# An order set by hand for VectorE, ScalarE, GpSimd and the loads in the paired output projection

## The chip, the cores and the metric

The kernel runs on one core of a Trainium2 chip. Its metric is device time in microseconds (us) of one execution. The core has TensorE (PE, the matrix unit), VectorE (DVE), ScalarE (ACT), GpSimd (POOL) and SyncE (SP, which here issues nearly all transfers); each runs its own instructions in order. On-chip data lie in SBUF, matrix results in PSUM, everything else in device memory.

## The reference

One encoder layer on 2048 tokens of width 1024: a modulated norm and a projection feed an attention branch and an mLSTM branch; their normed outputs are concatenated and go through one output projection into a gated residual; then comes a SwiGLU feed-forward with a second gated residual, and a last norm. The part this case is about, cut to what matters:

```python
att = rms_norm(att, g_attn_out)                                # width 512
h_m = sigmoid(o_m) * rms_norm(h_fwd + h_bwd, g_mlstm_out)      # width 512
mix = concatenate([att, h_m], axis=-1) @ w_out                 # 1024 x 1024
x = x + gate1 * mix
hff = rms_norm(x, g_norm2) * (1.0 + scale2) + shift2
gte, up = split(hff @ w_ffn_in, 2, axis=-1)
ff = (silu(gte) * up) @ w_ffn_out
return x + gate2 * ff
```

All values are 32-bit floats. A product of the kernel is made of three matrix instructions, on a high and a low part of each operand.

## The kernel before, in words

**Seven products instead of eight.** The output projection takes token tiles of 128 in pairs (8 pairs). A pair of tiles is seen as a 2 by 2 block matrix, tile by half of the 1024 input channels, and multiplied by the weight's four blocks in Strassen's manner: seven products u0 to u6 instead of eight. Each has four k-steps of three matmuls (lines 56, 57 and 58, tile `ops`), so a pair has 84 matmuls and 28 steps i. Three PSUM banks hold the results: u0, u2, u4 and u6 add into one (b1), u1 has its own (b2), u3 and u5 share the third (b5). After each product VectorE adds the bank to the residual row `xr` (L1033). A later product into the same bank may start only when that addition has read it: u2 waits for u0's addition, u4 for u2's, u6 for u4's, u5 for u3's.

**What a pair needs.** `Pair(p)` loads the pair's attention outputs twice (`msq`, to be squared, and `ma`), the mLSTM outputs (`mm`) and, in `load_gate`, the output gate (`og`). `sums` squares `msq` on ScalarE (L972) and sums it in two GpSimd steps (L973, L974); `root` has TensorE add over channels (tile `aps`, L980) and VectorE make the inverse root (nine short instructions and L983); `scale` has TensorE spread it (tile `arb`) and VectorE scale `ma` (L990); `gate` multiplies `mm` (L993). `operands` makes the seven left operands mA11, mA12, mS2, mS1, mS3, mS4 and mA22: four GpSimd sums or differences (L1006, L1007, L1012, L1015), and for each operand a ScalarE copy, the high part (L1001), and a VectorE subtraction, the low part (L1002). While pair p is multiplied, pair p+1 is scaled and its operands are made, and pair p+2 is loaded, squared and rooted.

**Ahead of the pairs** lies the fill: the products of the mLSTM output gate (`o_tiles`, L417, tile `gps`, copied to `oth` and stored to `og_d`), between which the first two pairs are prepared; `pull(n)` takes n of its steps. The output weights' seven products (`wo`, two tiles each for high and low) are loaded and finished there too (L889 load, L890 ScalarE copy, L891 VectorE subtraction).

**Beside the pairs** runs `norm2`, the second norm, for four token tiles at a time (in pairs 2, 3 and 4, 5, 6): it loads the new residual rows (`x1t`) that the pairs before have stored (L1037), squares them (`junk`, L1081), makes the inverse roots (`rs`), scales (L1086), transposes them on TensorE (`trn`, L162; ScalarE makes `n` from them, L163), and stores blocks to device memory (`hop_d`). The second group (z = 1) loads the first group's blocks back and stores their sums. In pair 7 `refill_ops` loads these blocks as the feed-forward's right operands (tiles `B` and `T`, finished at L1127 and L1128), and `weights` makes the feed-forward's first left operands (L1166, L1167). Then the feed-forward begins (tile `fp`; ScalarE copies `s` at L1263 and `u` at L1269 free its banks).

**What sets the order.** TensorE's order is written by hand, in the order of the program text, from the second half of the kernel on. VectorE, ScalarE, GpSimd and SP have theirs from the scheduler of the tile framework, which sets it at build time by its own costs. SP's queue is in order as well: a transfer that waits for its slot holds those behind it, and each transfer has to wait for the eighth before it.

Of the kernel before, what the change touches and what calls it, by code (L numbers as in the profile page):

```python
# [21 lines left out]
P = 128  # L22
# [14 lines left out]
def hybrid_layer_kernel(  # L37
# [844 lines left out]
    wo = []  # L882

    def load_wo(us):
        for u in us:
            hl = [[big(4 * u + 2 * z + i, "wo") for i in range(2)] for z in range(2)]
            for i in range(2):
                hi, lo = hl[0][i], hl[1][i]
                sp.dma_start(lo.bitcast(F32), wo_d[u, 2 * i:2 * i + 2].rearrange("k p t -> p k t"))  # L889
                act.activation(hi, lo.bitcast(F32), AF.Copy)  # L890
                dve.tensor_tensor(lo, lo.bitcast(F32), hi.bitcast(F32), SUB)  # L891
            wo.append(hl)
# [6 lines left out]
    for s_ in range(len(order) + 2):  # L899
# [24 lines left out]
        if len(wo) < 4 and s_ > 31 and lasts[len(wo) // 2] not in fill:  # L924
            load_wo(range(len(wo), len(wo) + 2))
    assert next(wops, None) is None
    finish_fill(lasts[1])
    load_wo(range(len(wo), 4))
# [21 lines left out]
    class Pair:  # L950


        def __init__(self, p):
            self.tt = tt = TO[2 * p]
            v = lambda t: t.rearrange("p i k t -> p (i k) t")
            self.sq = mring_tile("msq", F32).rearrange("p i (k t) -> p i k t", k=4)
# [11 lines left out]

        def sums(self):

            sq = self.sq
            act.activation(sq, sq, AF.Square)  # L972
            pool.tensor_tensor(sq[:, :, 0:2], sq[:, :, 0:2], sq[:, :, 2:4], ADD)  # L973
            pool.tensor_tensor(sq[:, :, 0], sq[:, :, 0], sq[:, :, 1], ADD)  # L974
# [20 lines left out]
        def operands(self):  # L995
# [9 lines left out]
            s2_ = xp.tile([P, 512], F32, tag="n2", name="ms2", bufs=5)  # L1005
# [33 lines left out]

    nxt = Pair(0)  # L1040
    nxt.load_gate()
    xr = [load_xr(nxt.tt + i) for i in range(2)]
    nxt2 = Pair(1)
    nxt.sums()
    nxt.gate()
    nxt2.load_gate()
    pull(36)
    finish_fill(lasts[1])
    nxt.root()
    nxt2.sums()  # L1050
    pull(18)
    nxt.scale()
    ready = nxt.operands()
    next(ready), next(ready), next(ready)
    finish_fill(lasts[2])
    load_wo(range(4, 6))
    pull(10)
# [3 lines left out]
    load_wo(range(6, 7))  # L1061
    deque(ready, 0)
# [5 lines left out]
    def norm2(hh, z, tags, lead):  # L1068
# [15 lines left out]
        yield True  # L1084
        for i in range(4):
            act.activation(xt[i], xt[i], AF.Copy, scale=r[:, i:i + 1])  # L1086
            yield True
        if z == 0:
            for k in range(KT):
                t = new()  # L1090
                turned(t, xt, k, tags[k % 2], gs2, mod[:, 3, :])
                sp.dma_start(op["B11" if k < 4 else "B21"][k % 4], t)
                yield True
        else:
            done = ()
            for k in range(4):
                for o, t in done:
                    sp.dma_start(op[o][k - 1], t)
# [5 lines left out]
                turned(b22, xt, k + 4, tags[1], gs2, mod[:, 3, :])  # L1104
                e.tensor_tensor(t3, b22, b12, SUB)
                dve.tensor_tensor(b12, b12, b11, SUB)
                dve.tensor_tensor(b11, b22, b12, SUB)
                e.tensor_tensor(b21, b21, b11, SUB)
                done = (("B22", b22), ("T3", t3), ("T1", b12), ("T2", b11), ("T4", b21))
                yield True  # L1110
            yield True
            for o, t in done:
                sp.dma_start(op[o][3], t)

    def refill_ops(hh):
# [14 lines left out]
        def after(u):  # L1130
            start(u)
            if u > 1:
                finish(u - 2)
# [3 lines left out]
    ring = deque([("big", "big28")] + [("w", f"w{i}{z}") for i in range(2) for z in "hl"]  # L1137
                 + [("big", f"big{i}") for i in range(29, 32)] + [("ff", f"r{i}") for i in range(4)])
# [20 lines left out]
    def weights(raw, early=False):  # L1159

        w11, w12, s2_, s1_, s3_, s4_, w22 = (ring_tile(n) for n in ("A11", "A12", "S2", "S1", "S3", "S4", "A22"))
        g, a21, a22 = raw
        a11, a12 = g[:, :512], g[:, 512:]

        def part(t, f):
# [7 lines left out]
        part(w11, a11)  # L1173
        part(w12, a12)
        part(s1_, f1)
        pool.tensor_tensor(a21, a11, a21, SUB)
        part(s2_, f2)
# [383 lines left out]
```

## Time and profile before

| | us |
|---|---|
| median of 3 runs | 2414.3 (2413.35 to 2416.13) |
| the profiled execution | 2406.27 |
| its span in the profile | 2404.5 |
| TensorE busy | 2265.9 |
| the eight pairs, first product to last | 883.8 to 1086.4 |

All times in the profile count from the start of the span. A row of the instruction view is start, length, engine, line, operation, output and inputs, shape, and in brackets how long the engine stood idle before it and whose work ended that. "SPq" is the issue of a transfer. The rows of waits give engine and line, what was waited for, and total, times and longest. A duration of a matmul row is longer than the spacing of two matmuls, since they overlap.

### The profile page before, as it was taken

What the parts mean: (1) busy time and instruction counts of PE and PEld (TensorE: products, weight loads), DVE (VectorE), ACT (ScalarE), POOL (GpSimd) and SP (SyncE); (2) the same over time, 40 slices, a digit from 0 to 9 for tenths busy, and PEclk for the clock granted to TensorE, in tenths of its full rate; (3) what the DMA queues carried; (4) which work ended last, traced back from release to release, by engine and by line L of the source; (5) the groups of instructions that cost most, each with busy time, mean ns of one, the idle gap of its engine ahead of it and who ended that gap; (6) DMA issues with size and microseconds to landing.
All of it is one profiled execution on the core that took longest, in us unless ns stands there. A gap on an engine that the chain in (4) does not pass through costs nothing.

```text
span 2404.5 us, 32677 instructions
## 1 busy us (share of the span) xinstructions
PE 2265.9 (94%) x10801; PEld 1874.7 (78%) x10801; DVE 1565.9 (65%) x3096; ACT 1061.2 (44%) x2133; POOL 1024.1 (43%) x874
## 2 busy tenths in 40 slices
PE   5988999999999978987999999999999999999998
PEld 4987777788787857766888888788888888888886
DVE  6774677767687756667555567756565537684684
ACT  4522555544577733435345344533344423223452
POOL 1001234334466332434655655555656545492020
PEclk9999999999999989998999999999999999999999
DMA  7573455576788576865334345633333264442452
GB/s 291 175 242 105 132 160 160 170 213 186 220 253 255 164 239 205 265 244 179 105 110 167 97 143 182 210 100 112 102 107 105 88 206 157 150 161 97 141 199 89
DMA packets 363522, 401.86 MB, mean 167 GB/s; under 512 B 24670, under 2 KB 255576, under 8 KB 363352
## 3 DMA queue, kind: packets, MB, share of 16 engines
q1 hardware_dynamic: 363352, 399.78, 52.5%
q8 instruction: 85, 1.39, 0.3%
q14 instruction: 85, 0.70, 0.1%
HBM read 280.50 MB, written 119.19 MB: 166 GB/s over the span
## 4 chain that ended last, share of the span: by engine, by line
PE 50%; DVE 4%; DMA 4%; POOL 3%; issue 2%; ACT 2%; SPq 1%; POOLq 0%; ACTq 0%; DVEq 0%
PE fp L56 11%; PE fp L57 11%; PE fp L58 11%; PE fo L58 5%; PE fo L56 5%; PE fo L57 5%; DMA msq<-mxa_d 1%; PE ops L56 1%; DVE al L1346 1%; PE gps L417 1%; DMA al<-a_d 1%; PE ops L57 1%; PE ops L58 1%; POOL ms L1007 0%; POOL ma L1006 0%
## 5 line engine op out<-in xcount | busy, mean ns | idle before, releaser
L417 PE MATMUL gps<-hT,whi 128*128 128x512 f32 x1088 | 401.7, 425 | 8.6 <-ACT ctanh L431 7.8
L56 PE MATMUL fo<-w,ah 128*128 128x512 f32 x616 | 242.2, 393 | 2.6 <-ACT ah L1345 2.6
L58 PE MATMUL fo<-w,al 128*128 128x512 f32 x616 | 242.4, 393 | 0.2 <-DVE al L1346 0.2
L57 PE MATMUL fo<-w,ah 128*128 128x512 f32 x616 | 241.9, 393 | 0.0
L417 PEld LDWEIGHTS gps<-hT,whi 128*128 128x128 f32 x1088 | 204.6, 194 | 35.9 <-ACT ctanh L431 8.5
L417 PE MATMUL gps<-hT,wlo 128*128 128x512 f32 x544 | 230.7, 424 | 0.0
L56 PE MATMUL fp<-T,S 128*128 128x512 f32 x528 | 210.0, 398 | 15.5 <-ACT s L1263 9.9
L57 PE MATMUL fp<-T,S 128*128 128x512 f32 x528 | 208.2, 394 | 0.0
L58 PE MATMUL fp<-T,S 128*128 128x512 f32 x528 | 208.2, 394 | 0.0
L1346 DVE TENSOR_TENSOR al<-al,ah 128x1024 fp32r<-128x1024 f32 x77 | 114.4, 1490 | 134.2 <-ACT ah L1345 133.9
L1167 DVE TENSOR_TENSOR A<-graw,A 128x512 fp32r<-128x512 f32 x86 | 105.4, 1246 | 108.0 <-ACT A L1166 108.0
L1345 ACT ACTIVATE ah<-al 128x1024 fp32r<-128x1024 f32 x77 | 81.6, 1060 | 193.8 <-DMA al<-a_d 184.7
L56 PEld LDWEIGHTS fo<-w,ah 128*128 128x128 f32 x616 | 115.8, 188 | 28.9 <-ACT ah L1345 3.0
L58 PE MATMUL fp<-B,A 128*128 128x512 f32 x352 | 137.6, 391 | 0.0
L56 PE MATMUL fp<-B,A 128*128 128x512 f32 x352 | 137.6, 391 | 0.0
L57 PE MATMUL fp<-B,A 128*128 128x512 f32 x352 | 137.6, 391 | 0.0
L58 PEld LDWEIGHTS fo<-w,al 128*128 128x128 f32 x616 | 115.8, 188 | 27.7 <-DVE al L1346 1.4
L57 PEld LDWEIGHTS fo<-w,ah 128*128 128x128 f32 x616 | 115.9, 188 | 26.4
L56 PEld LDWEIGHTS fp<-T,S 128*128 128x128 f32 x528 | 100.3, 190 | 39.3 <-ACT s L1263 10.8
L1167 DVE TENSOR_TENSOR S<-sf,S 128x512 fp32r<-128x512 f32 x86 | 87.5, 1019 | 55.9 <-ACT S L1166 55.8
L58 PEld LDWEIGHTS fp<-T,S 128*128 128x128 f32 x528 | 100.1, 190 | 22.6
L57 PEld LDWEIGHTS fp<-T,S 128*128 128x128 f32 x528 | 100.4, 190 | 21.7
(376 smaller groups left out, 6045.5 us busy)
## 6 DMA issues: line engine op xcount, KB each, us to landing
al<-a_d SPq DMA_DIRECT2D x77, 512.0 KB, 3.5
wmod<-in_w_mod_dram SPq DMA_DIRECT2D x48, 512.0 KB, 5.9
graw<-in_w_ffn_in_dram SPq DMA_DIRECT2D x43, 512.0 KB, 4.4
a_d<-ka SPq DMA_DIRECT2D x66, 256.0 KB, 2.3
bc<-bc_d SPq DMA_DIRECT2D x64, 256.0 KB, 4.1
hop_d<-n SPq DMA_DIRECT2D x56, 256.0 KB, 4.2
a_d<-u SPq DMA_DIRECT2D x55, 256.0 KB, 2.6
mqk<-qk_d SPq DMA_DIRECT2D x48, 256.0 KB, 3.5
```

Of the source, the lines that this page charges most:

```text
L56: pe.matmul(o, lh, rh, start=first, stop=False, skip_group_check=skip)
L57: pe.matmul(o, lh, rl, start=False, stop=False, skip_group_check=skip)
L58: pe.matmul(o, ll, rh, start=False, stop=last, skip_group_check=skip)
L417: pe.matmul(ps, w[i == 2][:, k, :], hT[n](i == 1, k), start=(k == 0 and i == 0), stop=(k == KT - 1 and i == 2))
L1167: dve.tensor_tensor(t[:, 1, :], f, t[:, 0, :].bitcast(F32), SUB)
L1345: act.activation(ah, al.bitcast(F32), AF.Copy)
L1346: dve.tensor_tensor(al, al.bitcast(F32), ah.bitcast(F32), SUB)
```

## The change

1. `load_wo` is cut into `start_wo` (loads) and `finish_wo` (copies and subtractions). The loads of products 2 and 3 start early in the fill and are finished at its end; those of 4, 5 and 6 are finished in pair 0 at steps 4, 8 and 12.
2. From the fill's end to the end of the eight pairs, VectorE, ScalarE, GpSimd and SP also run in the order of the program text.
3. In that text: the squares of pairs 0 and 1 have a place of their own (the slots of `x1t`), the buffer `ms2` too; squaring is cut from the sums; the gate is at step 2, the operands at steps 5, 7, 10, 13, 16, 19 and 23, the square at 9, the sums at 11, the root at 17, loads of `xr` at 6 and 25.
4. The fill is taken in other portions: 8, 14, 16, 8, 10, 14 steps with the preparation of pairs 0 and 1 between.
5. `norm2` is taken a step further at every odd i (14 a pair) and no longer at every third; one of the z = 1 stores comes a step later.
6. The first weights of the feed-forward are loaded in pair 6 and made in pair 7, one part at each of seven steps; the refill is finished three products later instead of two. In the feed-forward the ring of slots starts elsewhere, and the second early operand for the last matrix product comes behind u3.

The diff, cut to its core:

```diff
+    def start_wo(u):
+        hl = [[big(4 * u + 2 * z + i, "wo") for i in range(2)] for z in range(2)]
+        wo.append(hl)
+        for i in range(2):
+            sp.dma_start(hl[1][i].bitcast(F32), wo_d[u, 2 * i:2 * i + 2].rearrange("k p t -> p k t"))
+
+    def finish_wo(u):
+        for hi, lo in zip(*wo[u]):
+            act.activation(hi, lo.bitcast(F32), AF.Copy)
+            dve.tensor_tensor(lo, lo.bitcast(F32), hi.bitcast(F32), SUB)
...
-            self.sq = mring_tile("msq", F32).rearrange("p i (k t) -> p i k t", k=4)
+            sq = mring_tile("msq", F32) if p > 1 else xp.tile([P, 2, 512], F32, tag="xt", name="msq", bufs=4)
+            self.sq = sq.rearrange("p i (k t) -> p i k t", k=4)
...
+    rest = ExitStack()
+    rest.enter_context(tc.manual_schedule(engines={getattr(mybir.EngineType, e) for e in ("DVE", "Activation", "Pool", "SP")}))
     nxt = Pair(0)
     nxt.load_gate()
-    xr = [load_xr(nxt.tt + i) for i in range(2)]
+    xr = [load_xr(nxt.tt)]
+    finish_fill(lasts[1])
+    pull(8)
+    nxt.square()
+    for u in (2, 3):
+        start_wo(u)
+    nxt.sums()
+    pull(14)
+    nxt.root()
+    nxt.gate()
+    xr.append(load_xr(nxt.tt + 1))
     nxt2 = Pair(1)
+    pull(16)
+    nxt.scale()
...
+    start_wo(6)
+    for u in (2, 3):
+        next(ready)
+        finish_wo(u)
...
+    OPERANDS = (5, 7, 10, 13, 16, 19, 23)
+    FIRST = (1, 2, 5, 8, 10, 14, 18)
     for p in range(NT // 2):
...
         for i in range(28):
             pull(1)
+            if p == 0 and i in (4, 8, 12):
+                next(left)
+                finish_wo(i // 4 + 3)
...
-                elif i in (6, 9, 12, 15, 18, 21, 24):
+                elif i in OPERANDS:
                     next(ready)
...
-            elif i == 2:
-                nxt_w = weights(load_raw(0, True), True)
+            else:
+                if i == 0:
+                    first_w = weights(first_raw, True)
+                if i in FIRST:
+                    nxt_w = next(first_w)
             if nxt2:
-                if i == 10:
+                if i == 9:
+                    nxt2.square()
+                elif i == 11:
                     nxt2.sums()
                 elif i == 17:
                     nxt2.root()
-            if norms and i % 3 == 1 and next(norms[0], None) is None:
+            elif nxt and i == 20:
+                first_raw = load_raw(0, True)
+            if norms and i % 2 and next(norms[0], None) is None:
                 norms.popleft()
         while fill:
             pull()
+    rest.close()
...
         def last_ops(u):
-            if u < 2:
-                finish_op(u + 5)
+            if u < 3:
+                finish_op(u + 4)
...
-        early = [operands("A11", k) for k in range(2)]
-        pair(1, JO[0], nxt_w, hop)
+        early = [operands("A11", 0)]
+        pair(1, JO[0], nxt_w, hop, lambda u: early.append(operands("A11", 1)) if u == 3 else None)
```

In the rows below a number behind a name only tells buffers apart. VectorE in pair 1, before; `ma_10511` and `mm_10512` belong to pair 2, `ops_10684` and `ops_10685` are the banks b1 and b2 of pair 1:

```order
L1033 TENSOR_TENSOR xr_10277<-xr_10277,ops_10517 128x512
L990 SCALAR_TENSOR_TENSOR ma_10511<-ma_10511,cols_86,arb_10693 128x2x128 x4
L1033 TENSOR_TENSOR xr_10572<-xr_10572,ops_10684 128x512
L1002 TENSOR_TENSOR mA12_10735<-mm_10512,mA12_10735 128x512
L1002 TENSOR_TENSOR mA11_10722<-ma_10511,mA11_10722 128x512
L1002 TENSOR_TENSOR mS2_10754<-ms2_10710,mS2_10754 128x512
L1033 TENSOR_TENSOR xr_10572<-xr_10572,ops_10685 128x512
L1002 TENSOR_TENSOR mS1_10768<-ma_10511,mS1_10768 128x512
L1033 TENSOR_TENSOR xr_10572<-xr_10572,ops_10684 128x512
```

The same place now (`ma_10492`, `mm_10493` of pair 2; `ops_10686`, `ops_10687` are b1 and b2 of pair 1):

```order
L995 SCALAR_TENSOR_TENSOR ma_10492<-ma_10492,cols_86,arb_10695 128x2x128 x4
L998 SCALAR_TENSOR_TENSOR mm_10493<-og_10522,mm_10493 128x1024
L1038 TENSOR_TENSOR xr_10546<-xr_10546,ops_10686 128x512
L1007 TENSOR_TENSOR mA11_10721<-ma_10492,mA11_10721 128x512
L1038 TENSOR_TENSOR xr_10546<-xr_10546,ops_10687 128x512
L1007 TENSOR_TENSOR mA12_10733<-mm_10493,mA12_10733 128x512
L1007 TENSOR_TENSOR mS2_10747<-ms2_10712,mS2_10747 128x512
L1038 TENSOR_TENSOR xr_10546<-xr_10546,ops_10686 128x512
```

The addition for u1 (b2) stood behind mS2 and now stands ahead of mA12 and mS2; the next addition into b1, for u2, follows mS2 directly. GpSimd in pair 1, before; `msq_10677` is pair 3's, `ma_10511` pair 2's:

```order
L973 TENSOR_TENSOR msq_10677<-msq_10677 128x2x256
L974 TENSOR_TENSOR msq_10677<-msq_10677 128x2x128
L1006 TENSOR_TENSOR ma_10511<-ma_10511 128x512
L1007 TENSOR_TENSOR ms2_10710<-mm_10512,ma_10511 128x512
L1015 TENSOR_TENSOR mm_10512<-mm_10512,ms2_10710 128x512
L1012 TENSOR_TENSOR ma_10511<-ms2_10710,ma_10511 128x512
```

and now, with `msq_10679` of pair 3 and `ma_10492` of pair 2:

```order
L1011 TENSOR_TENSOR ma_10492<-ma_10492 128x512
L1012 TENSOR_TENSOR ms2_10712<-mm_10493,ma_10492 128x512
L1017 TENSOR_TENSOR ma_10492<-ms2_10712,ma_10492 128x512
L1020 TENSOR_TENSOR mm_10493<-mm_10493,ms2_10712 128x512
L978 TENSOR_TENSOR msq_10679<-msq_10679 128x2x256
L979 TENSOR_TENSOR msq_10679<-msq_10679 128x2x128
```

The two sums of pair 3's squares moved from ahead of pair 2's four operand steps to behind them. ScalarE in pair 2, before; `x1t_10869` and `x1t_10870` are tiles of `norm2`'s first group, the squares `msq_10844` pair 4's:

```order
L972 ACTIVATE msq_10844<-msq_10844 128x1024
L1001 ACTIVATE mA12_10910<-mm_10679 128x512
L1001 ACTIVATE mA11_10897<-ma_10678 128x512
L1001 ACTIVATE mS2_10932<-ms2_10885 128x512
L1001 ACTIVATE mS1_10948<-ma_10678 128x512
L1001 ACTIVATE mS3_10983<-ma_10678 128x512
L1081 ACTIVATE junk_10954,ssq_10922<-x1t_10869 128x1024
L1081 ACTIVATE junk_10990,ssq_10922<-x1t_10870 128x1024
```

and now, where `x1t_10869` and `x1t_10870` are the first two tiles of that group:

```order
L1006 ACTIVATE mA11_10896<-ma_10680 128x512
L1006 ACTIVATE mA12_10908<-mm_10681 128x512
L1100 ACTIVATE junk_10913,ssq_10912<-x1t_10869 128x1024
L973 ACTIVATE msq_10846<-msq_10846 128x1024
L1100 ACTIVATE junk_10922,ssq_10912<-x1t_10870 128x1024
L1006 ACTIVATE mS2_10927<-ms2_10887 128x512
```

Two of `norm2`'s squares and pair 4's square now stand ahead of mS2. VectorE at the end of the fill and in pair 0, before, up to the first residual addition:

```order
L1002 TENSOR_TENSOR mA12_10391<-mm_10268,mA12_10391 128x512
L891 TENSOR_TENSOR wo_10408<-wo_10408,wo_10406 128x1024
L1002 TENSOR_TENSOR mS1_10498<-ma_10267,mS1_10498 128x512
L891 TENSOR_TENSOR wo_10486<-wo_10486,wo_10484 128x1024
L1002 TENSOR_TENSOR mS4_10504<-mm_10268,mS4_10504 128x512
L990 SCALAR_TENSOR_TENSOR ma_10280<-ma_10280,cols_86,arb_10526 128x2x128
L891 TENSOR_TENSOR wo_10487<-wo_10487,wo_10485 128x1024
L990 SCALAR_TENSOR_TENSOR ma_10280<-ma_10280,cols_86,arb_10526 128x2x128 x3
L1033 TENSOR_TENSOR xr_10275<-xr_10275,ops_10517 128x512
```

and now, from the operand mS2 of pair 0 on:

```order
L1007 TENSOR_TENSOR mS2_10476<-ms2_10356,mS2_10476 128x512
L893 TENSOR_TENSOR wo_10270<-wo_10270,wo_10268 128x1024
L893 TENSOR_TENSOR wo_10271<-wo_10271,wo_10269 128x1024
L1007 TENSOR_TENSOR mS1_10484<-ma_10236,mS1_10484 128x512
L893 TENSOR_TENSOR wo_10276<-wo_10276,wo_10274 128x1024
L893 TENSOR_TENSOR wo_10277<-wo_10277,wo_10275 128x1024
L995 SCALAR_TENSOR_TENSOR ma_10321<-ma_10321,cols_86,arb_10507 128x2x128 x4
L998 SCALAR_TENSOR_TENSOR mm_10322<-og_10354,mm_10322 128x1024
L1038 TENSOR_TENSOR xr_10244<-xr_10244,ops_10498 128x512
```

Four subtractions of the weights of products 2 and 3 and the gate of pair 1 stand ahead of that addition now; the six of products 4 to 6 follow behind it.

More of the change, by code (lines that the diff above doesn't have):

```diff
@@ L923, in hybrid_layer_kernel @@
         u2, u1 = u1, u0
[L924 to L928, printed above, removed]
+        if not wo and s_ > 31 and lasts[0] not in fill:
+            for u in range(2):
+                start_wo(u)
+    assert next(wops, None) is None and wo
+    for u in range(2):
+        finish_wo(u)
     s3s.close()
```

103 lines of the change are left out of this document (50 added, 53 removed).

## The prediction

> **What bounds the kernel now.** I read the profile's summary first, then the waits of TensorE around the stage, then the stage cut into its pairs, and last the single instructions at the places where TensorE stood.
>
> ```profile
> span 2404.5 us, 32677 instructions
> PE 2265.9 (94%) x10801; PEld 1874.7 (78%) x10801; DVE 1565.9 (65%) x3096; ACT 1061.2 (44%) x2133; POOL 1024.1 (43%) x874
> ```
>
> TensorE is busy 94% of the span, and the change removes no matrix product. All that it can win is idle time of TensorE. The waits, in three stretches (841 to 884 us is the fill ahead of pair 0, 884 to 1090 the eight pairs, then the start of the feed-forward); the columns are total, times, longest:
>
> ```profile
> PE aps L980 <- POOL msq L974: 9.1, 2, 4.8
> ...
> PE ops L56 <- DVE xr L1033: 19.3, 7, 4.0
> PE trn L162 <- ACT n L163: 5.7, 2, 5.1
> ...
> PE fp L56 <- ACT s L1263: 9.9, 2, 5.7
> PE fp L56 <- ACT u L1269: 3.2, 1, 3.2
> ```
>
> So 9.1 us lie before the pairs, 25.0 in them and 13.1 behind them: 47.2 us in all. The eight pairs, cut at their first product (columns: length, then busy time of PE, PEld, DVE, ACT and POOL, TensorE's granted clock, DMA share, GB/s; pair 3 left out):
>
> ```profile
> 883.80:912.10 28.30, 23.33 (x93) 18.31 (x94) 23.13 (x40) 10.24 (x15) 12.63 (x8) 0.88 0.66 202
> 912.10:936.90 24.80, 20.77 (x89) 16.79 (x88) 15.46 (x33) 7.12 (x12) 8.30 (x6) 0.93 0.63 211
> 936.90:961.90 25.00, 22.46 (x102) 18.21 (x102) 16.15 (x46) 11.43 (x16) 8.33 (x6) 1.00 0.66 221
> ...
> 986.90:1011.70 24.80, 23.28 (x113) 19.11 (x111) 16.41 (x46) 12.69 (x20) 8.43 (x6) 1.00 0.94 309
> 1011.70:1036.60 24.90, 20.94 (x94) 17.08 (x93) 16.45 (x34) 8.71 (x13) 10.49 (x7) 0.93 0.49 165
> 1036.60:1067.20 30.60, 24.92 (x112) 20.05 (x112) 18.22 (x25) 8.54 (x13) 16.36 (x12) 0.89 0.81 289
> 1067.20:1086.40 19.20, 19.20 (x86) 15.73 (x84) 15.02 (x18) 11.41 (x14) 3.22 (x3) 1.00 0.90 339
> ```
>
> Pair 7 is the floor: its seven products (84 matmuls) without a wait take 19.2 us, 2.74 a product. The others carry transposes or norm sums beside (their x) and wait 1.5 to 5 us. A long wait costs more than itself. Behind a wait of 4.03 us the clock is low, behind one of 2.5 us it is not:
>
> ```profile
> 927.80:932.30 4.50, 4.50 (x16) 3.69 (x17) 2.69 (x11) 1.65 (x4) 0.00 (x0) 0.69 0.41 120
> 952.10:954.60 2.50, 2.48 (x13) 2.14 (x14) 1.90 (x5) 1.78 (x5) 0.00 (x0) 1.00 0.16 41
> ```
>
> So a wait near 4 us costs 4.5 × (1 − 0.69) = 1.4 us on top.
>
> **Fill and first sums.** The squares of pair 0 are loaded behind four loads of weights (issue, landing as the start of the square, the sums, TensorE):
>
> ```profile
> 842.76 1.04 SPq L889 DMA_DIRECT2D wo<-wo_d  x2
> ...
> 846.57 0.53 SPq L960 DMA_DIRECT2D msq<-mxa_d  x1
> ...
> 854.28 1.06 ACT L972 ACTIVATE msq<-msq 128x1024 f32<-128x1024 f32 x1 [0.73 <-DMA msq<-mxa_d]
> ...
> 857.54 1.01 PE L980 MATMUL aps<-ones_r,msq 128*128 128x1 f32 x4 [4.84 <-POOL msq L974]
> 871.63 0.61 PE L980 MATMUL aps<-ones_r,msq 128*128 128x1 f32 x4 [4.29 <-POOL msq L974]
> ...
> 848.00:866.00 18.00, 13.16 (x52) 10.63 (x51) 8.59 (x22) 5.67 (x6) 1.98 (x2) 0.81 1.13 333
> ```
>
> Now this load stands ahead of those four, which began at 842.76, 3.8 us earlier; with the same chain the sums would be ready at 853.7. But TensorE also comes to them earlier, after 23 matmuls of the fill and not 37. It waited from 852.7 (857.54 less 4.84); since 842, 37 matmuls are 0.29 us each, so it stands there at 848.7. If the load lands as slowly as before (7.7 us from issue to the square) the wait stays near 5; if it lands in 4, it is 1.3. I take 3. The second pair's squares come behind about 5.75 MB (eleven and a half half-megabyte transfers in SP's order), which at 333 GB/s are 17.3 us: landing near 860, sums near 865, TensorE, 52 matmuls on, there near 866.8. GpSimd has three operand steps of pair 0 ahead of these sums now (1.3 to 1.8 us each), so the wait lies between 0 and 6; I take 2.5. Against 9.1 that is −3.6, and some 1.4 of clock from one long wait less: −5, between −12 (both gone, clock whole) and +1. The Trainium skill (DMA: Bandwidth & Descriptors, Specifications) gives the 16 engines together 435 GB/s for transfers of 512 bytes and more. By it, as an estimate, those 5.75 MB take 13 us, and this term is −8; the row at a full share shows 333, so the measurement decides and I keep −5.
>
> **Pair 0.** The finishing of weights 2 to 6 (one ScalarE copy and one VectorE subtraction for each of 10 tiles) moves from the fill into the last products and pair 0. Before, four such subtractions lay there. One took
>
> ```profile
> 883.30 1.23 DVE L891 TENSOR_TENSOR wo<-wo 128x1024 fp32r<-128x1024 f32 x1 [0.26 <-ACT wo L890]
> ...
> 885.64 2.31 DVE L891 TENSOR_TENSOR wo<-wo 128x1024 fp32r<-128x1024 f32 x1
> ```
>
> alone and beside GpSimd. Four stand on VectorE ahead of pair 0's first residual addition, with the scaling and the gate, and u2 waits for that addition (same accumulator). Six more at 1.23 are 7.4 us of VectorE in a pair where it was busy 23.1 of 28.3; at 2.31 they are 13.9. About a third of it reaches TensorE, since VectorE had 5.2 us free: I take +2.5, between −3 (the wait of before goes and all hides) and +8 (13.9 less 5.2). The Trainium skill (GPSIMD Engine Reference, 1. Specifications) says GpSimd shares its SBUF interfaces with VectorE and contends with VectorE's instructions of two SBUF inputs. The subtraction is one, and the pair of rows agrees. By that rule with all six beside GpSimd, this term is +8.
>
> **Pairs 1 and 3.** Here is the wait in pair 1, on GpSimd, VectorE, ScalarE and TensorE:
>
> ```profile
> 917.13 1.30 POOL L973 TENSOR_TENSOR msq<-msq 128x512 f32<-128x512 f32 x1 [15.84 <-ACT msq L972]
> 918.50 1.06 POOL L974 TENSOR_TENSOR msq<-msq 128x256 f32<-128x256 f32 x1
> 919.52 1.73 POOL L1006 TENSOR_TENSOR ma<-ma 128x512 f32<-128x512 f32 x1
> 921.34 1.29 POOL L1007 TENSOR_TENSOR ms<-mm,ma 128x512 f32<-128x512 f32 x1
> ...
> 914.66 1.65 DVE L990 SCALAR_TENSOR_TENSOR ma<-ma,cols,arb 128x256 f32<-128x256 f32 x4
> ...
> 923.33 1.22 DVE L1002 TENSOR_TENSOR mS<-ms,mS 128x512 fp32r<-128x512 f32 x1 [3.22 <-ACT mS L1001]
> ...
> 926.97 0.68 DVE L1033 TENSOR_TENSOR xr<-xr,ops 128x512 f32<-128x512 f32 x1
> ...
> 927.80 0.76 PE L56 MATMUL ops<-wo,mS 128*128 128x512 f32 x1 [4.03 <-DVE xr L1033]
> ```
>
> GpSimd could have begun L1006 at 916.3, when the scaling ended, but stood in order behind the sums of the pair after next, whose squares landed at 916. So mS2 came 3.2 us late, and VectorE had it ahead of the addition that TensorE waited for. The hand order mends both: the sums go behind all four of GpSimd's operand steps, and the additions of u0 and u1 ahead of mS2. The wait of 4.03 and its 1.4 go: at best −5.4 in pair 1, where mA22 now needs a slot that the next pair's arb frees, for which I leave 1.9: −3.5. Pair 3 takes −3 by the same reading, less because it carries transposes beside. Bounds: −5.4 and 0 each.
>
> **Pairs 2 and 4.** These start norm2 for a group of tokens. SP is in order: the last store of the pair before, msq, ma, two mm, then four x1t; on ScalarE the first two norm squares (junk) stand ahead of mS2. Before, they stood behind it, or a tile had been loaded a pair earlier. How such a burst lands, at pair 4 (issue, then ScalarE waiting for tiles 1 and 3):
>
> ```profile
> 997.65 1.84 SPq L1072 DMA_DIRECT2D x1t<-x_d  x4
> ...
> 1001.19 1.06 ACT L1081 ACTIVATE junk<-x1t 128x1024 bf16<-128x1024 f32 x1 [1.04 <-DMA x1t<-x_d]
> ...
> 1004.10 1.06 ACT L1081 ACTIVATE junk<-x1t 128x1024 bf16<-128x1024 f32 x1 [0.20 <-DMA x1t<-x_d]
> ```
>
> The first tile lands 3.5 us after issue, the third 6.4. Issued about 3 us into the pair behind 1.5 MB more (4.5 us at 333 GB/s), tile 1 lands 10 to 11 us in and tile 2 at 12; mS2 then follows (1.1 of junk, 0.7 of ScalarE, 0.7 of VectorE) at 14.5, and behind it the addition that u4 waits for, which by the floor's pace (four products) would start at 11. So a wait of 3 to 4.5 replaces the one of 2.5 here (in pair 4 a shorter one, by its busy 23.28 of 24.80). I take +1.5 for each, between −2.5 (the wait goes) and +6 (4.5 more and the clock's 1.4).
>
> **Pairs 5 and 6.** Here the second group's blocks go through memory and back: a step loads two tiles into slots that a store two transfers earlier must free.
>
> ```profile
> 1052.62 1.12 PE L162 MATMUL trn<-ident,x1t 128*128 128x128 f32 x4 [5.14 <-ACT n L163]
> ...
> SPq L1098 <- ACT n L163: 22.6, 3, 15.8
> ```
>
> Pair 6 loses 5.14 and its clock so; pair 5, by its clock of 0.93, waits as pair 1 does. Stepping at every second call, not every third, brings more of this chain into pair 5 and its waits earlier; their releaser, a landing, stays. Best −12 (both waits with their clock), worst +3; I take −5, half of the best. Pair 7 has no wait to lose: 0, although its first weight sums now stand ordered by hand among its additions.
>
> **Feed-forward.** Before its first copy s ScalarE still finishes six weight halves:
>
> ```profile
> 1091.37 1.99 ACT L1127 ACTIVATE T<-T 128x1024 fp32r<-128x1024 f32 x2
> 1093.26 1.99 ACT L1127 ACTIVATE B<-B 128x1024 fp32r<-128x1024 f32 x2
> 1095.16 1.99 ACT L1127 ACTIVATE T<-T 128x1024 fp32r<-128x1024 f32 x2
> ```
>
> In the new order they and some norm squares still stand ahead of s, since this part is scheduled again and not by hand. The first two weight sums are spared it, though, and the second early operand moves behind u3. Of 13.1 I take −4, between −13 and +2.
>
> **Sum:** −5 + 2.5 − 3.5 − 3 + 1.5 + 1.5 − 5 + 0 − 4 = −15 us. The profiled execution took 2406.27, 8 us under the median of 2414.3; differences carry over, so 2414.3 − 15 = 2399.
>
> **Rivals.**
> - Nearly all waits go: −12 in the fill, −5.4 and −3 in pairs 1 and 3, −2.5 twice, −12, −8: −45, so 2369. For it: every wait has a releaser that did other work first. Against it: in pairs 2, 4, 5 and 6 that other work now waits for landings.
> - Slower: ScalarE, in order, holds parts behind tiles that have not landed. Place: mS2 in pairs 2 and 4, the n copies in 5 and 6. Price at its end: +6, +6 and +3, instead of +1.5, +1.5 and −5, which is +17 to the sum: +2; with pair 0's +8, +8, so 2422. It decides when those four pairs together take over 15 us more than I took, or 9.5 with pair 0 at its bound. For it: DMA's share is 0.94 in pair 4 already, so landings can be later than in the rows.
> - It does nothing that lasts: what the pairs lose the fill and the feed-forward give, within 5 us: 2414.
>
> **Chances.** The forecast's case (−5 to −30) 0.48, nearly all waits gone 0.16, nothing 0.11, slower 0.25. A change under 0.2%, 4.8 us, can't be told from none here. So faster 0.64, same 0.11, slower 0.25. The range of the likeliest case is 2385 to 2409; 8 in 10 reach from 2370 to 2426.
>
> **What would show it.** Right: the chain of waits has TensorE's wait for the addition in pair 1 gone; GpSimd's L1011 right behind the scaling; in pairs 2 and 4 a wait of TensorE for the addition, with ScalarE's junk before it waiting for x1t; the first product 3 to 8 us earlier. Wrong: pairs 2 and 4 under 22 us (x1t lands early), pair 0 over 34 (weights), a first wait of the feed-forward that is gone or doubled.

## The result: 0.5 to 0.7% slower, and the profile after

The changed kernel took 2431.1 us in the median (2429.7 to 2434.3) against 2415.2 before; the ratio is 1.0068, 95% interval 1.0050 to 1.0085. Measured a second time beside other kernels it took 2422.9 against 2412.5, ratio 1.0048 (1.0030 to 1.0066). So it is slower by 10 to 16 us, where 15 us faster was forecast. Single executions of one kernel differ by 5 to 18 us here: the kernel before ran from 2402.8 to 2421.3 in one batch. Between the two profiles of the changed kernel (2429.5 and 2421.3 us) 6 of the 8 us lie ahead of the stage (over all profiles the last attention transpose lies between 834 and 845 us). So the parts below are compared by their own lengths. One of the six executions of the kernel measured last, "the same again", fell into a slow state (2538.6 us, clock 0.845) and is left out of its numbers.

TensorE is busy for 2271.0 us of the span after (93%), against 2265.9 before, with the same 10801 instructions.

TensorE's waits after, in the same three stretches as in the prediction (columns: total, times, longest):

```profile
PE gps L417 <- ACT oth L489: 5.1, 1, 5.1
PE aps L985 <- POOL msq L979: 2.7, 2, 2.3
...
PE ops L56 <- DVE xr L1038: 29.7, 8, 7.8
PE trn L162 <- ACT n L163: 5.4, 2, 5.0
PE ops L56 <- ACT mA L1006: 4.8, 1, 4.8
...
PE fp L56 <- ACT s L1302: 8.7, 1, 8.7
```

The waits for sums fell from 9.1 to 2.7, but one of 5.1 for a copy (oth) came instead. In the pairs the wait for the residual additions grew from 19.3 to 29.7. The pairs after, cut near the first matmul of u0 (columns as in the prediction, pair 7 left out). The borders lie up to 0.6 us, three matmuls, beside that matmul, so the length of a single pair is good to about 0.6 us:

```profile
884.80:920.20 35.40, 23.70 (x93) 18.43 (x92) 31.68 (x46) 17.18 (x23) 10.54 (x6) 0.86 0.38 121
920.20:943.80 23.60, 20.87 (x95) 16.65 (x94) 16.27 (x34) 5.89 (x9) 9.96 (x6) 1.00 0.59 182
943.80:973.70 29.90, 22.32 (x93) 18.13 (x92) 16.83 (x45) 13.46 (x20) 8.71 (x6) 0.89 0.62 210
973.70:998.20 24.50, 24.10 (x125) 19.70 (x124) 14.85 (x33) 10.82 (x16) 8.41 (x6) 1.00 0.80 257
998.20:1028.40 30.20, 22.36 (x95) 18.19 (x94) 16.82 (x45) 13.47 (x20) 8.71 (x6) 0.89 0.62 211
1028.40:1063.40 35.00, 26.98 (x123) 21.81 (x122) 18.92 (x39) 9.34 (x14) 16.61 (x12) 0.85 0.75 251
1063.40:1088.60 25.20, 22.13 (x93) 17.79 (x92) 16.43 (x22) 7.09 (x11) 14.86 (x10) 0.93 0.92 320
```

The same cut shows a fault in the prediction's own table: its borders between pairs 1 and 5 were set about evenly and not at the first matmul. Cut as above, pairs 1 to 5 before took 25.8, 23.0, 25.7, 23.2 and 26.8 us. Pairs 2 and 4 before:

```profile
937.90:960.90 23.00, 20.46 (x94) 16.56 (x93) 15.81 (x45) 10.43 (x16) 8.33 (x6) 1.00 0.65 224
...
986.60:1009.80 23.20, 21.68 (x103) 17.76 (x102) 16.02 (x45) 10.88 (x20) 8.43 (x6) 1.00 0.93 307
```

They were shorter than the 25.0 and 24.8 of the prediction's table. TensorE's idle time in them is the same under either cut (2.5 and 1.5 us), and so is the sum of the pairs.

| part, us | before | after | after, second measurement |
|---|---|---|---|
| last attention transpose to first product | 46.1 | 41.1 | 41.3 |
| pair 0 | 28.3 | 35.4 | 35.4 |
| pairs 1 and 3 | 25.8 + 25.7 | 23.6 + 24.5 | 23.0 + 24.4 |
| pairs 2 and 4 | 23.0 + 23.2 | 29.9 + 30.2 | 30.4 + 30.3 |
| pairs 5 and 6 | 26.8 + 30.6 | 35.0 + 25.2 | 34.9 + 25.2 |
| pair 7 | 19.2 | 19.1 | 19.2 |
| all pairs | 202.6 | 222.9 | 222.8 |
| first feed-forward matmul to the end | 1318.1 | 1321.8 | 1319.6 |

The fill won 5 us, the pairs lost 20, the feed-forward 1.5 to 3.7. The two measurements agree to 0.6 us in every pair.

**Where pairs 2 and 4 lost.** Pair 2 began at 943.8. Its chain, by SP, ScalarE, VectorE and TensorE:

```profile
951.04 2.19 SPq L1091 DMA_DIRECT2D x1t<-x_d  x4
...
957.38 1.06 ACT L1100 ACTIVATE junk<-x1t 128x1024 bf16<-128x1024 f32 x1 [7.96 <-DMA x1t<-x_d]
958.43 1.04 ACT L973 ACTIVATE msq<-msq 128x1024 f32<-128x1024 f32 x1
959.38 1.04 ACT L1100 ACTIVATE junk<-x1t 128x1024 bf16<-128x1024 f32 x1
...
960.42 0.61 ACT L1006 ACTIVATE mS<-ms 128x512 fp32r<-128x512 f32 x1
...
961.07 1.10 DVE L1007 TENSOR_TENSOR mS<-ms,mS 128x512 fp32r<-128x512 f32 x1 [9.06 <-ACT mS L1006]
962.09 0.67 DVE L1038 TENSOR_TENSOR xr<-xr,ops 128x512 f32<-128x512 f32 x1
...
962.91 0.77 PE L56 MATMUL ops<-wo,mS 128*128 128x512 f32 x1 [7.58 <-DVE xr L1038]
```

ScalarE stood 7.96 us before a norm square whose tile had not landed. Behind it in order stood mS2, on VectorE the addition behind mS2's low part, and TensorE behind the addition. The four loads were issued 7.2 us into the pair, behind msq, ma and mm. SP stood 2.0 us ahead of the first mm, whose slot GpSimd's L1011 had still to release; the issue of ma took 1.6 us more:

```profile
SPq L965 <- POOL ma L1011: 2.0, 1, 2.0
```

**Where pair 5 lost.** ScalarE stood before a slot that a store must free:

```profile
1046.02 0.78 ACT L163 ACTIVATE n<-trn,mod,gs 128x512 f32<-128x512 f32 x1 [11.66 <-DMA hop_d<-n]
...
1048.30 0.63 ACT L1006 ACTIVATE mS<-ms 128x512 fp32r<-128x512 f32 x1
...
1048.96 0.69 DVE L1007 TENSOR_TENSOR mS<-ms,mS 128x512 fp32r<-128x512 f32 x1 [7.73 <-ACT mS L1006]
...
1046.85 1.12 PE L162 MATMUL trn<-ident,x1t 128*128 128x128 f32 x4 [5.00 <-ACT n L163]
1050.30 0.79 PE L56 MATMUL ops<-wo,mS 128*128 128x512 f32 x1 [2.34 <-DVE xr L1038]
```

**Where pair 0 lost.** VectorE was busy 31.7 of its 35.4 us. Its work on the output weights, and the two waits of TensorE that end at the additions behind it:

```profile
890.04 2.35 DVE L893 TENSOR_TENSOR wo<-wo 128x1024 fp32r<-128x1024 f32 x2
892.32 1.65 DVE L995 SCALAR_TENSOR_TENSOR ma<-ma,cols,arb 128x256 f32<-128x256 f32 x4
893.88 1.21 DVE L998 SCALAR_TENSOR_TENSOR mm<-og,mm 128x1024 f32<-128x1024 f32 x1
895.02 0.68 DVE L1038 TENSOR_TENSOR xr<-xr,ops 128x512 f32<-128x512 f32 x1
...
903.27 4.48 DVE L893 TENSOR_TENSOR wo<-wo 128x1024 fp32r<-128x1024 f32 x2
...
895.84 0.76 PE L56 MATMUL ops<-wo,mS 128*128 128x512 f32 x1 [4.82 <-ACT mA L1006]
909.62 0.77 PE L56 MATMUL ops<-wo,mS 128*128 128x512 f32 x1 [6.58 <-DVE xr L1038]
```

The profile puts the first of these waits down to ScalarE's mA, an operand of the next pair, which this matmul does not read; the addition for u0, which it needs, ended at 895.70.

### The profile page after: what moved, and what is told of

Its sections match the earlier page's. It is cut to its first block, busy times and chain, and to the rows that moved or that the text cites. A ratio compares the mean times of both kernels' runs of the same rounds, so it can differ in the third digit from the quotient of the medians.

```text
span 2429.5 us, 32711 instructions
## 1 busy us (share of the span) xinstructions
PE 2271.0 (93%) x10801; PEld 1876.6 (77%) x10801; DVE 1579.1 (65%) x3096; ACT 1060.9 (44%) x2133; POOL 1029.5 (42%) x874
## 4 chain that ended last, share of the span: by engine, by line
PE 52%; DVE 5%; DMA 4%; issue 2%; ACT 1%; POOL 1%; SPq 1%; DVEq 0%; ACTq 0%; POOLq 0%
PE fp L56 11%; PE fp L58 11%; PE fp L57 11%; PE fo L58 5%; PE fo L57 5%; PE fo L56 5%; PE ops L56 1%; PE ops L57 1%; PE ops L58 1%; DMA hop_d<-n 1%; DMA x1t<-x_d 1%; DMA al<-a_d 1%; PE gps L417 1%; SPq L965 0%; DVE wo L893 0%
## 5 line engine op out<-in xcount | busy, mean ns | idle before, releaser
L58 PEld LDWEIGHTS fo<-w,al 128*128 128x128 f32 x616 | 115.8, 188 | 29.9 <-DVE al L1385 3.5
L56 PEld LDWEIGHTS fp<-T,S 128*128 128x128 f32 x528 | 100.2, 190 | 38.3 <-ACT s L1302 13.4
```

Of the source, the lines that this page charges most:

```text
L56: pe.matmul(o, lh, rh, start=first, stop=False, skip_group_check=skip)
L58: pe.matmul(o, ll, rh, start=False, stop=last, skip_group_check=skip)
```

## The experiments

Theory H: an engine in order stands before work that is not ready (a landing, a slot), and ready work behind it holds TensorE. The rivals are named with each run. All edits are made to the changed kernel unless said otherwise. The column of all pairs is exact (first matmul of pair 0 to first matmul of the feed-forward); single pairs are good to about 0.6 us, as above.

| run | median, us | ratio to before (95%) | all pairs, us | from the feed-forward on, us |
|---|---|---|---|---|
| changed kernel, first and second | 2431.1, 2422.9 | 1.0068 (1.0050 to 1.0085), 1.0048 (1.0030 to 1.0066) | 222.9, 222.8 | 1321.8, 1319.6 |
| norm squares late | 2410.2 | 0.9987 (0.9977 to 0.9998) | 203.7 | 1320.8 |
| x1t loads first | 2424.8 | 1.0052 (1.0036 to 1.0068) | 220.1 | 1320.8 |
| weights finished in the fill | 2416.5 | 1.0018 (1.0002 to 1.0035) | 215.5 | 1320.0 |
| scheduler's order | 2406.0 | 0.9966 (0.9949 to 0.9983) | 198.0 | 1320.7 |
| squares late, weights in the fill | 2404.1 | 0.9971 (0.9959 to 0.9983) | 196.8 | 1322.0 |
| and the hop chain spread | 2392.7 | 0.9925 (0.9902 to 0.9948) | 194.2 | 1318.5 |
| the same again | 2394.5 | 0.9935 (0.9913 to 0.9958) | 194.6 | 1319.3 |
| all three, scheduler's order | 2406.4 | 0.9980 (0.9965 to 0.9994) | 201.8 | 1320.6 |
| all three, squares six calls late | 2405.9 | 0.9977 (0.9964 to 0.9990) | 194.9 | 1325.6 |
| norm2 as before | 2420.1 | 1.0027 (1.0007 to 1.0048) | 214.4 | 1320.1 |
| refill as before | 2421.7 | 1.0035 (1.0021 to 1.0049) | 222.1 | 1316.8 |

**The control.** The changed kernel, unedited.

> The changed kernel itself, unedited, beside the others of this batch, since the time up to the stage differed by 3 to 6 us between profiles. If the edits alone made the differences: 2431 again (2428 to 2434). If part of them was the chip or the hour: 2422 to 2427, and the edits are worth that much less.

It took 2422.9, in the second case: 8 us of the distance of every edit's total to 2431 were not the edit's. The kernel before moved by less than 3 us between the batches (2412.4 to 2415.2), so why the changed kernel moved by 8 stays open. Its pairs repeated to 0.6 us each, so the verdicts below rest on the pairs.

**Norm squares late.**

```diff
-            norms.append(norm2(0, p // 2 - 1, "bd", 3))
+            norms.append(norm2(0, p // 2 - 1, "bd", 8))
```

> One edit: norm2 waits for eight calls instead of three before its first square, so on ScalarE its squares (junk) come at steps 17 to 23, behind mS2 (step 10), and not ahead of it. Theory H (ScalarE stands in order before a tile that has not landed, and mS2, the additions and TensorE stand behind it): pairs 2 and 4 fall from 29.9 and 30.2 us to 22 to 24 each, the rest within 1.5 us each, total 12 to 15 us under the changed kernel, so 2416 to 2419. Rival L (the transfers themselves are too slow: mS2's own chain waits for ma and mm in these pairs): pairs 2 and 4 stay at 29 to 30 and the total at 2431.

Pairs 2 and 4 fell to 21.0 and 22.0, further than expected, and the clock was whole. Their rows:

```profile
940.90:961.90 21.00, 20.62 (x93) 16.50 (x92) 17.27 (x41) 9.34 (x16) 9.47 (x6) 1.00 0.89 300
984.50:1006.50 22.00, 20.47 (x94) 16.68 (x93) 15.84 (x36) 9.31 (x16) 9.02 (x6) 1.00 0.90 304
```

ScalarE in pair 2 of this run:

```profile
949.78 0.62 ACT L1006 ACTIVATE mS<-ms 128x512 fp32r<-128x512 f32 x1
...
954.30 1.06 ACT L1100 ACTIVATE junk<-x1t 128x1024 bf16<-128x1024 f32 x1 [2.85 <-DMA x1t<-x_d]
```

The tile came as late in the pair as without the edit (13.4 us in; 13.6 in the changed kernel), and ScalarE still waited for it. But mS2 was done by then, so nothing of TensorE's stood behind. Theory H holds; the rival, that the transfers as such are too slow, falls. The price of a wait of 7.6 us was 8.9 (29.9 to 21.0): TensorE's idle time in the pair fell by 7.2, and its 93 instructions, as many as before the edit, were busy for 1.7 us less, at a clock of 1.00 and no longer 0.89. The total, 2410.2, is 13 us under the control.

**x1t loads first.**

```diff
-            norms.append(norm2(0, p // 2 - 1, "bd", 3))
+            norms.append(norm2(0, p // 2 - 1, "bd", 4))
+            next(norms[0])
```

> One edit: the four loads of x1t are issued ahead of the next pair's msq, ma and mm, at the head of the pair, and the squares stay ahead of mS2 on ScalarE. Theory H: the wait is for the landing, so it shortens by what the loads come earlier, less the landing of the last store that they wait for: tile 1 lands 8 to 9 us into the pair and not 13.6, the waits of 7.6 and 7.8 us fall to 1 to 4, total 6 to 12 us under 2431. Rival: the order on ScalarE alone costs the time, whenever the tiles land: waits stay over 6 us, total within 3 us of 2431.

Neither case: the waits fell only to 6.44 and 5.85 us, and all pairs by 2.8 us together. The total, 2424.8, is no lower than the control. The reason is a second landing in the same row of work:

```profile
948.91 1.06 ACT L1100 ACTIVATE junk<-x1t 128x1024 bf16<-128x1024 f32 x1 [2.18 <-DMA x1t<-x_d]
...
954.59 1.06 ACT L973 ACTIVATE msq<-msq 128x1024 f32<-128x1024 f32 x1 [4.53 <-DMA msq<-mxa_d]
```

The tile came 8 us into the pair (it began at 941.1), as expected, but msq, now loaded behind, was waited for next, and its square stands ahead of mS2 as well. A wait of an engine in order goes to whatever lands last ahead of the work that matters. The expectation had looked at one of the two.

**Weights finished in the fill.**

```diff
     next(ready), next(ready)
+    for u in (2, 3):
+        finish_wo(u)
     finish_fill(lasts[2])
...
     nxt2.root()
+    for u in (4, 5):
+        finish_wo(u)
     while fill:
         pull()
     start_wo(6)
-    for u in (2, 3):
-        next(ready)
-        finish_wo(u)
+    next(ready), next(ready)
...
                 next(left)
-                finish_wo(i // 4 + 3)
+                if i == 8:
+                    finish_wo(6)
```

> One edit: the weights of products 2 to 5 are finished (ScalarE copy, VectorE subtraction) in the fill, where ScalarE stood idle, and only product 6 in pair 0. Theory: pair 0's 35.4 us are VectorE's work on weights ahead of the additions; without eight of the ten subtractions pair 0 takes 24 to 28 us, total 7 to 11 us under 2431 if the fill does not get longer. Rival: VectorE is slowed by GpSimd's operand steps in any case and the additions wait for mS2 anyway: pair 0 stays over 32 us. A second rival: the subtractions take the time in the fill instead (first product later by 5 us or more), total unchanged.

Pair 0 took 28.2, the fill 41.3 as in the changed kernel: 7.2 us won, nothing given back, at the edge of what was expected. Pair 0 is with that no better than before the change (28.3). One wait remains, behind the two subtractions left there:

```profile
890.72 4.50 DVE L893 TENSOR_TENSOR wo<-wo 128x1024 fp32r<-128x1024 f32 x2
...
897.09 0.77 PE L56 MATMUL ops<-wo,mS 128*128 128x512 f32 x1 [5.87 <-DVE xr L1038]
```

These two took 2.25 each, where the median of the ten is 1.22: GpSimd was at an operand step (L1020) and at sums (L978, L979) from 890.3 to 895.8. In the changed kernel, too, the three of the ten that took about 2.3 us (at 896.7, 903.3 and 905.5) are the three that ran beside such steps of GpSimd. The Trainium skill (GPSIMD Engine Reference, 1. Specifications) says that GpSimd's SBUF interfaces are shared with VectorE, with contention where a VectorE instruction has two SBUF inputs; this subtraction has two, and the rows agree with it.

**Scheduler's order.**

```diff
     rest = ExitStack()
-    rest.enter_context(tc.manual_schedule(engines={getattr(mybir.EngineType, e) for e in ("DVE", "Activation", "Pool", "SP")}))
```

> One edit: VectorE, ScalarE, GpSimd and SP are ordered by the scheduler again; all else of the change stays. If the hand order is the cause: pairs 2 and 4 near 25 us, pairs 5 and 6 near 55 together, total 2408 to 2418. If the text's other changes (steps of norm2, where weights are finished and loaded) are the cause, whatever sets the order: 2425 to 2435.

2406.0, under all that was expected, and faster than the kernel before by 0.2 to 0.5%. So the other parts of the change, taken together and in the scheduler's order, are a small gain, and the order by hand turns it into a loss. TensorE's waits in its pairs:

```profile
PE ops L56 <- DVE xr L1038: 10.2, 6, 2.8
PE trn L162 <- ACT n L163: 4.2, 3, 1.8
PE ops L56 <- ACT junk L1099: 3.5, 1, 3.5
PE aps L985 <- POOL msq L979: 2.9, 1, 2.9
```

They sum to 20.8 us, where those of the changed kernel sum to 41.3; that is most of the 25 us between their pairs. The profile puts one of them, 3.5 us in pair 4, down to a norm square (junk), which that matmul does not read. The addition that it needs ended just ahead of it, behind pair 5's gate:

```profile
995.17 1.22 DVE L998 SCALAR_TENSOR_TENSOR mm<-og,mm 128x1024 f32<-128x1024 f32 x1
996.30 0.68 DVE L1038 TENSOR_TENSOR xr<-xr,ops 128x512 f32<-128x512 f32 x1
```

**Norm2 as before**, in the hand order: its old text, and a step at every third i.

> The changed kernel with norm2 and its step as before (every third step, a first square at step 10, behind mS2), in the hand order. Theory H: pairs 2 and 4 near 21 to 24 us; pairs 5 and 6, where the chain's steps are 9 apart and not 8, near 55 to 60 together; total 10 to 18 us under the changed kernel. Rival: what costs is that the order is fixed by hand at all: pairs 2 and 4 stay at 27 or more.

Pairs 2 and 4 took 23.1 and 22.0, as theory H has it. Pairs 5 and 6 took 25.4 + 40.1 = 65.5, more than the 55 to 60 expected: with steps 9 apart, the same slot is waited for in pair 6 three times. ScalarE there:

```profile
1048.67 1.45 ACT L163 ACTIVATE n<-trn,mod,gs 128x512 f32<-128x512 f32 x2 [11.86 <-DMA hop_d<-n]
1055.86 0.78 ACT L163 ACTIVATE n<-trn,mod,gs 128x512 f32<-128x512 f32 x1 [5.74 <-DMA hop_d<-n]
...
1064.88 0.78 ACT L163 ACTIVATE n<-trn,mod,gs 128x512 f32<-128x512 f32 x1 [5.89 <-DMA hop_d<-n]
```

So the closer step of the change alone was not what cost in pairs 5 and 6: with steps of 9 they took longer than with steps of 8. The old text also places its stores otherwise, so the two lengths can't be told apart by this run. With both, ScalarE waited for a store. The total, 2420.1, is 11 us under the first measurement, as expected, but only 3 under the control.

**Squares late and weights in the fill together.**

> Two edits together: norm2's squares eight calls late, and the weights finished in the fill. If they act in different pairs, as theory H has it, they add up: pairs 0, 2 and 4 at 28, 22 and 22 us, total 7 us under the first edit alone, so 2400 to 2405. Rival: one wait hides the other (what is saved in pair 0 comes back in the first norm sums or loads of pair 1): total 2408 or more.

The pairs took 28.3, 23.3, 21.0, 23.7, 20.9, 28.7, 31.5 and 19.2, and the total 2404.1: the two add up (203.7 less 7.2 is 196.5, measured 196.8).

**And the hop chain spread**: a third edit on top of these two, in norm2's second group, whose blocks hop through device memory (hop_d).

```diff
                 sp.dma_start(b21, op["B21"][k])
+                yield True
                 turned(b12, xt, k, tags[0], gs2, mod[:, 3, :])
...
                 sp.dma_start(op["T4"][k], b21)
+                if k < 3:
+                    yield True
```

> The two edits together, and a third: each of the four steps of the second group's chain through memory takes six calls instead of four, with one between the loads and the transposes and one behind the last store. Theory H for pairs 5 and 6: ScalarE's n copies stand in order before a slot that a store must free, ahead of the operands; given 12 steps and not 8 the store has landed: pairs 5 and 6 together fall from 59 to 48 to 53 us, total 5 to 11 us under the two edits. Rival: the store's landing (some 10 us around) is longer than a step in any case, so the wait moves to pair 6: together 57 or more, total unchanged.

Pairs 5 and 6 together took 47.1 us against 60.2, more than expected, and 50.3 in the second measurement. But pair 7 rose from 19.2 to 27.7 and 26.2, so that the pairs as a whole won 2.6 us. What ScalarE's n copies waited for a freed slot in pairs 5 and 6 of the changed kernel (total, times, longest):

```profile
ACT n L163 <- DMA hop_d<-n: 23.1, 3, 11.7
```

The same of this kernel, in its second measurement:

```profile
ACT n L163 <- DMA hop_d<-n: 2.8, 1, 2.8
```

And what the later chain met in pair 7 of it, at GpSimd's first weight sum:

```profile
1055.81 1.29 POOL L1195 TENSOR_TENSOR sf<-A,A22r 128x512 f32<-128x512 f32 x1 [7.42 <-DMA hop_d<-n]
```

Its slot is one of the chain's; the sum's parts stand on VectorE ahead of an addition, and TensorE waited 5.43 us there.

**The same again.**

> The kernel with the three edits once more, unchanged, since its four times (2389 to 2402) lie 11 us under those of the two edits while its pairs take only 2.6 us less. If the pairs tell all: eight pairs 194 to 195 us together again, total 2395 to 2406. If there is more to it than the pairs: 2388 to 2394 again.

2394.5, pairs 194.6: between the two cases by the total, the first by the pairs. This kernel is faster than before by 0.4 to 1.0%, and 28 to 30 us faster than the changed one in its second measurement. The totals are 10 and 11 us under the two edits' while the pairs are only 2 to 3 under. Some 3 us more lie behind the pairs (1318.5 and 1319.3 against 1322.0): TensorE's waits at the feed-forward's start sum to 8.1 and 7.6 us, against 10.4 with two edits. The remainder lies ahead of the stage, in code that no edit touches, and stays open.

**All three, squares six calls late.**

> The three edits, with norm2's squares six calls late instead of eight (steps 13 to 19, still behind mS2). With eight, pair 7 took 27.7 us and not 19.2: GpSimd's first weight sums waited for a slot that the chain's last store had to free, and held VectorE's additions. Theory H, fourth place: two calls (four steps, 2.7 us) earlier shorten that wait of 6.35 us to 2 to 4, pair 7 to 21 to 25 us, total 2 to 7 us under the 2392.7 of the three edits. Rival: the store's landing sets itself by its load and its slot (10 us around a step), not by the call: pair 7 stays over 26.

Pair 7 fell to 19.5, under what was expected, and GpSimd's wait ahead of its first weight sum to 1.2 us. But pairs 2 and 6 rose (24.8 and 24.3, from 21.0 and 21.5), so that the pairs as a whole stayed at 194.9, and the part behind them took 1325.6: the total was 2405.9, eleven us or more worse than with eight calls. The mechanism in pair 7 is shown, the forecast of a gain was wrong: the waits moved to other places. In the feed-forward TensorE waited a second time for a copy s, 5.3 us at 1121.5, which it did not do with eight calls; on ScalarE three of norm2's scalings (L1108) and two operand copies lay just ahead of that copy. Why the scheduler, which orders this part, put them there stays open.

**All three, scheduler's order.**

> The three edits, with the scheduler's order for VectorE, ScalarE, GpSimd and SP. If the scheduler's gain over the hand order was only that it did not place waiting work ahead (theory H), then with these edits the hand order is as good: this run within 5 us of the hand order with the same three edits. If the scheduler's order is better for another reason too: 8 us or more under it.

2406.4, 12 to 14 us behind the same text in the hand order, and no better than the scheduler's order without these edits. Neither expected case came: the hand order is ahead. By the pairs, which repeat better, it wins 7 us (194.2 and 194.6 against 201.8). By the totals only one of its two texts wins: with the squares six calls late it took 2405.9, as much as the scheduler's order. So the scheduler's order has no advantage of its own here, and in the pairs the hand order is the better one once its unready work is moved back.

**Refill as before.**

```diff
-            if u > 2:
-                finish(u - 3)
+            if u > 1:
+                finish(u - 2)
...
-            if u < 3:
-                finish_op(u + 4)
+            if u < 2:
+                finish_op(u + 5)
```

> The changed kernel with one part undone: the refill is finished two products after its load again, and only its last two products' operands in the feed-forward. The part from the feed-forward's first matmul to the end took 1319.6 and 1321.8 us in the changed kernel and 1318.1 before. If the refill's later finishing is the cause (the wait of 8.7 us for s): that part 2 to 5 us shorter, the wait 5 to 6, pair 7 within 2 us of 19.2. Rival: in the hand order of pair 7 an operand finished sooner waits for its landing on ScalarE and holds the parts behind it: pair 7 over 22 us and nothing won. Second rival: something else in that part (waits of later units) took the time: the first wait shrinks, the part stays.

The part from the feed-forward on took 1316.8, 3 to 5 us less than in the changed kernel, with pair 7 at 19.2 still; the wait for s fell to 7.2 only. So the later refill did cost, but by less of that wait than thought. The total hardly moved (2421.7 against 2422.9).

## Why the prediction was wrong, step by step

It forecast 2399 (faster), and the ratio says slower by 0.3 to 0.85%. The mechanism that decided is the one it named as its rival on the slower side, with a chance of 0.25: ScalarE, in order, holds parts behind tiles that have not landed. Its sign came true as well: the four pairs 2, 4, 5 and 6 together took 18.7 us more than the forecast had for them, and it had asked for 15.

- **Fill, −5: right** in its sum (46.1 to 41.1), not in its parts, so the sum is in part luck. The waits for sums fell to 0.44 and 2.30, but one of 5.11 for oth appeared that no step of the prediction had:

```profile
855.92 0.61 PE L985 MATMUL aps<-ones_r,msq 128*128 128x1 f32 x4 [0.44 <-POOL msq L979]
873.38 0.79 PE L417 MATMUL gps<-hT,whi 128*128 128x512 f32 x1 [5.11 <-ACT oth L489]
...
872.73 0.60 ACT L489 ACTIVATE oth<-gps 128x512 f32<-128x512 f32 x1 [9.10 <-DMA og_d<-oth]
```

  The copy oth waits for its slot's store, which SP had behind the loads of pair 1. Again work behind a landing. The 2.30 has the same cause: on ScalarE the square of pair 1 stood right behind that copy, at 873.23.
- **Pair 0, +2.5: mis-sized**, measured +7.1. "About a third of it reaches TensorE" was the failing step. All the work lies on the one engine whose additions TensorE waits for, twice in the pair, 4.8 and 6.6 us; the bound of +8 (by its own numbers, 13.9 less 5.2, rather 8.7) was near. Pair 0's 35.4 us met the prediction's sign of being wrong, over 34.
- **Pairs 1 and 3, −3.5 and −3: right in kind**, measured −2.2 and −1.2. The wait of 4.03 went. The gain is smaller since TensorE still waits 1.4 for an addition and 1.4 for sums, and pair 3 took on more transposes (125 TensorE instructions where 116 were).
- **Pairs 2 and 4, +1.5 each: the failing step.** Measured +6.9 and +7.0, over the end given. The working had the chain right, and its own times (tile 1 at 10 to 11 us, the addition at 14.5) come to a wait of 3 to 4.5. The size of the wait was wrong. The loads were issued 7.2 us into the pair, not 3, since SP stood ahead of mm and took longer over ma and mm than reckoned. Tile 1 was ready at 13.6, and the waits were 7.6 and 7.8. And the slow clock that follows such a wait was priced only in the bound of +6, not in the +1.5. As measured, TensorE's idle time rose by 5.0 us in pair 2 and 6.3 in pair 4 (which had only 1.5 us to give up), and its busy time by 1.9 and 0.7. The uneven borders of the table played no part, since these terms were read from waits.
- **Pairs 5 and 6, −5: wrong in sign**, +2.8. "Their releaser, a landing, stays" was written and then half of the best case taken all the same. All five slots are used in every step, so a step has to wait for a store and a load in a row; in pair 5 ScalarE stood 11.7 us before such a slot, ahead of an operand. Given six calls a step and no longer four, pairs 5 and 6 took 47 to 50 us.
- **Pair 7, 0: right.**
- **Feed-forward, −4: wrong in sign**, +1.5 to +3.7. The waits at its start fell as forecast (13.1 to 8.7), but later units waited (3.8, 1.9 and 2.2 us in the second measurement); the waits of the whole part are no less, 22.9 and 20.5 against 20.8. The other part is busy time of TensorE, 1290.8 us against 1288.6. The refill's delay is worth 3 to 5 us, by the run above. Why the busy time rose stays open.

The sum of the terms as measured, −5 + 7.1 − 2.2 − 1.2 + 6.9 + 7.0 + 2.8 + 2, is +17, a little over the medians' 16 and well over the 10 of the second measurement. The kernel before has one profile only, of an execution 8 us under its median, so its parts can be somewhat short; the signs of the terms for pairs 0, 2 and 4 do not hang on that, since each loss went with its edit. The larger mistake was one of weights: three terms were set between bounds at what the edit would bring if its new waits were short, although in each of them the row showed a landing that nothing made shorter.

## What to carry to other kernels

When an order is fixed by hand, ask of each instruction not only whether it is early enough but what it can wait for: anything that waits for a transfer, or for a slot that a transfer frees, must stand behind all work that the bound engine needs within that transfer's time. Moving such an instruction five calls back was worth 19 us of the pairs here, while making its transfer earlier was worth 3. And cut stretches at the instruction that begins them; here an uneven cut did no harm only because the terms were read from waits and not from lengths.

## What the runs showed that was not expected

- A stall's place is set by the last landing ahead of the work that matters: with one tile nearly 6 us earlier, another tile's landing took over, and TensorE's wait fell by 1.1 and 2.0 us only.
- A wait of 7.6 us cost 8.9, with the clock that follows it. But the traces give no sharp length at which the clock falls: behind waits of 2.95 us (before, pair 3) and 3.27 us (all three edits, first measurement, pair 5) it stayed at 1.00 for the next 4.5 us, and behind waits of 2.00 us (squares six calls late, pair 2) and 2.78 us (scheduler's order, pair 2) it fell to 0.62 and 0.68.
- The same text in the hand order and in the scheduler's differed by 12 to 14 us in one direction with the unready work moved back eight calls, and by 17 to 25 us in the other without.
